# Hard-max attention on one core: key differences made by one VectorE subtraction and one store, in place of a negated first key, three stores and an accumulating DMA

## The chip, the cores and the metric

One core of a Trainium2 chip runs the program. The metric is the device time in microseconds, the median of several executions. Engines are named as in the profile: PE (TensorE, matmuls), PEld (its weight loads), DVE (VectorE), ACT (ScalarE), POOL (GpSimd) and SP (SyncE). DMAs that POOL issues go through the queue q0 (software_dynamic), those that SP issues through q1 (hardware_dynamic).

## The reference

```python
B, Sq, Sk, D = 4, 4096, 4096, 128          # q, k, v: randn, float32

def reference(q, k, v):
    logits = np.matmul(q, k.transpose(0, 2, 1))
    best = np.argmax(logits, axis=-1)
    b_idx = np.arange(q.shape[0])[:, None]
    return v[b_idx, best, :].astype(np.float32)
```

For each query the output is the row of `v` whose key has the largest dot product with it.

## The kernel before

**Screening.** The 4 x 4096 queries are worked as 128 tiles of 128 queries, `NQT` = 32 tiles to a batch `b`. Keys are taken in groups of four. For each tile `t`, PE multiplies the queries with sums and differences of the keys of a group (`kT`, fp16), ACT takes absolute values (`A`, L222) and one rectified half (`E`, L235), PE adds `A` back in, and DVE folds the two halves into one word per group (`fold`, L248, tile `W`). A word holds the score in its upper half and the group's number in its lower half. `top` (L252) takes the eight largest words of each query. The score is a measure that the largest dot product in the group can't exceed by much, so the best word names the group in which the winner lies.

**Dots.** `gather` (L264 and L270) decodes the best word into `cand` on DVE and lets POOL issue one indirect DMA for each tile. It fetches for each of 128 queries three rows from a scratch array in DRAM, `k16[b]`: the differences of keys 1, 2 and 3 of the group to key 0, in fp16, 384 values in all. They land in a tile `kg`, of which there are `NKG` = 6. `dots` (L288 to L298) multiplies them with the queries and sums, and `pick` (L308 to L321) chooses the key by the largest of 0 and the three. POOL then fetches the row of `v` (`vr`, L328), and SP stores it (L333). Groups of tiles whose result is too near to call are flagged and worked exactly, once for the first half of the tiles, beside the loop, and once at the end (L468 on).

**The loop and its order.** The order on every engine is written out by hand: a loop over `it` from 0 to 127 issues loads, one unit of transposed keys for the next batch (`unit_k`), the matmuls of tile `it` and the end of tile `it - 1` (`screen`), the fold of tile `it - 1`, one step of each piece of work in progress (`step`), the maximum of tile `it - 2` (`top`), another step, and last the gathers (`gathers`, `issue`). Each engine works its list in order, and each DMA queue is issued in order. POOL's list has the loads of the keys and queries of later batches (`load_part`, L66 and L69), the gathers of `kg` and `vr`, and L94. SP's list has the stores of `k16`, `rec` (L341, the eight words of each query) and the output, and the transposing DMAs of the queries (`turn_q`, L196).

**How `k16` is made.** The keys of a batch lie in `natk[b % 2]` as fp16, 16 consecutive keys to a partition, in two halves `h`. For batch 0, `put_k` (L71 to L78) subtracts key 0 from keys 1 to 3 of each group on DVE, into `kd`, and SP stores the half in one DMA. For batches 1 to 3 the work is split in the loop:

- at tiles 9 and 13 of the batch before (`it % NQT in (9, 13)`, L787), between `fold` and `step`, `put_first` writes minus key 0 to `kd[:, h, :, 0, :]` on DVE (L84), and SP stores this into all three places of each group in `k16` (L87, three DMAs)
- at tiles 12 and 16 (L789), `add_rest` lets POOL issue one DMA from `natk` to `k16` with `accum_op=OP.add` (L94), which adds keys 1 to 3 to what lies there.

In both ways `k16` holds the same three differences. `kd` has two halves, so a store of one half has to be done before the next batch writes that half again. The first reader of `k16[b]` is the gather for the first tiles of batch `b`.

Of the kernel before, what the change touches and what calls it, by code (L numbers as in the profile page):

```python
# [15 lines left out]
OP = mybir.AluOpType  # L16
# [13 lines left out]
def kernel(ctx, tc, q, k, v, out):  # L30
    nc = tc.nc
    B, Sq, D = q.shape
    Sk = k.shape[1]
    P = 128
    NQT = Sq // P
# [21 lines left out]
    k16 = [dr.tile([Sk, 96], FP16, name=f"k16_{b}") for b in range(B)]  # L57
    kT = [bp.tile([P, Sk], FP16, name=f"kT{i}", tag=f"kT{i}") for i in range(2)]
    qT = [bp.tile([P, Sq], FP16, name=f"qT{i}", tag=f"qT{i}") for i in range(2)]
    natk = [bp.tile([P, 2, 16, P], FP16, name=f"natk{i}", tag=f"natk{i}") for i in range(2)]  # L60
    kd = bp.tile([P, 2, 4, 3, P], FP16, name="kd", tag="kd")
# [9 lines left out]
    def put_k(b, h):  # L71
        if b >= B:
            return
        src = natk[b % 2][:, h].rearrange("p (g f) d -> p g f d", f=4)
        nc.vector.tensor_tensor(out=kd[:, h], in0=src[:, :, 1:4, :], in1=src[:, :, 0:1, :].to_broadcast([P, 4, 3, P]),
                                op=OP.subtract)
        kb16 = k16[b].rearrange("(h p n) d -> p h (n d)", p=P, n=16)
        nc.sync.dma_start(out=kb16[:, h], in_=kd[:, h].rearrange("p g f d -> p (g f d)"))  # L78

    def put_first(b, h):  # L80
        if b >= B:
            return
        src = natk[b % 2][:, h].rearrange("p (g f) d -> p g f d", f=4)
        nc.vector.tensor_scalar(out=kd[:, h, :, 0, :], in0=src[:, :, 0, :], scalar1=-1.0, scalar2=None, op0=OP.mult)  # L84
        kb16 = k16[b].rearrange("(r x) d -> r (x d)", x=4).rearrange("(h p g) (f d) -> p h g f d", h=2, p=P, f=3)
        for f in range(3):
            nc.sync.dma_start(out=kb16[:, h, :, f, :], in_=kd[:, h, :, 0, :])  # L87

    def add_rest(b, h):
        if b >= B:  # L90
            return
        src = natk[b % 2][:, h].rearrange("p (g f) d -> p g f d", f=4)
        kb16 = k16[b].rearrange("(r x) d -> r (x d)", x=4).rearrange("(h p g) (f d) -> p h g f d", h=2, p=P, f=3)
        nc.gpsimd.dma_start(out=kb16[:, h].rearrange("p g f d -> p g (f d)"), in_=src[:, :, 1:4, :].rearrange("p g f d -> p g (f d)"),  # L94
                            accum_op=OP.add)

    def load_part(b, i):
        if b >= B:
            return
        if i < 8:  # L100
            load_k(b, i // 4, i % 4 * 4, i % 4 * 4 + 4)
        else:
            load_q(b, (i - 8) * NQT // 8, (i - 7) * NQT // 8)
# [91 lines left out]
    def turn_q(b, x, y):  # L195
        nc.sync.dma_start_transpose(out=qT[b % 2][:, x * P:y * P].rearrange("p (t r) -> p t r", r=P),  # L196
                                    in_=natq[b % 2][:, x:y, :].rearrange("p t d -> p (t d)"))
# [42 lines left out]
    def screen(t):  # L240
        dpart(t, 0)
        spart(t - 1, 0)
        dpart(t, 1)
        spart(t - 1, 1)

    def fold(t):
        E, ps = E_t.pop(t)
        nc.vector.scalar_tensor_tensor(out=W_t[t % NW].bitcast(I16)[:, 1::2], in0=ps, scalar=QSCALE, in1=E,  # L248
                                       op0=OP.mult, op1=OP.max)

    def top(t):
        nc.vector.max(out=TOP[:, t, :], in_=W_t[t % NW].bitcast(FP32))  # L252
# [433 lines left out]
    def step(it):  # L686
        quick = it >= TAIL
        waiting = [s for s in live if s["kind"] == "dots" and ready(s, it)]
        quota = 2 if len(waiting) > 1 else 1
        again = []  # L690
        for s in list(live):
            if s["kind"] == "dots":
                if quota and advance(s, it, False):
                    quota -= 1
            elif advance(s, it, False) and (quick or s["kind"] == "flags"):
                again.append(s)
        for s in again:
            if s in live:
                advance(s, it, False)
# [17 lines left out]
    def issue(it):  # L717
        n = 0
        clock[0] = it
        put_out(it)  # L720
        behind = len([g for g in near_q if g not in marks]) > (2 if it >= TAIL else 4)
        while near_q and (n < 1 + behind or near_q[0] in marks):
            g = near_q.pop(0)
            n += g not in marks
            g()
        if fast and it >= rest[0]:
            fast.pop(0)()
            rest[0] = it + 2
            n += 1
        if it < 16:  # L730
            take_late(2 if n == 0 and len(late_q) > 4 else 1)
            return
        b, qt = it // NQT, it % NQT
        busy = 0.4 if 10 <= qt < 18 and b + 1 < B or 18 <= qt < 26 and b + 2 < B else 0.0
        room[0] = min(room[0] + 2.42 - busy, 3.0) - n
        for i in range(2):
            if room[0] >= 1 and late_q:
                take_late(1)
                room[0] -= 1
# [3 lines left out]
    def gathers(t):  # L743
        for c, (t0, t1) in enumerate(chunks):
            m = 4 if t1 <= T - 56 else 2 if t < T - 2 else 1
            if t0 <= t < t1 and (t - t0) % m == m - 1:
                gather(c, t - m + 1, m)
            if t == t0:
                start(pick(c, t0, t1), "pick", c)
        if t % 8 == 7:  # L750
            put_rec(t - 7, t + 1)
        if t == SEGS[1] - 1:
            last = [c for c, x in enumerate(chunks) if x[1] == t + 1][0]
            start(flag_segment(0, t + 1, lambda: ("cnt", last) in done, lambda: ("out", last) in done), "flags")
# [3 lines left out]
    for b in range(1, B):  # L758
        x = b * NQT
        units += [(x - 1, x - NQT + (6 + 3 * i // 2 if b == 1 else 1 + 2 * i), unit_k, b, i) for i in range(16)]  # L760
    for it in range(T):
        b, qt = it // NQT, it % NQT
        if it < 8:
            load_part(1, it)
        elif 10 <= qt < 18:
            load_part(b + 1, qt - 2)
        elif 18 <= qt < 26:
            load_part(b + 2, qt - 18)
        open_units = [u for u in units if u[1] <= it]
        if open_units:  # L770
            u = min(open_units)
            units.remove(u)
            assert it <= u[0]
            u[2](*u[3:])
        if it == 1:
            turn_q(0, 4, 8)
        if it in (1, 2, 3):
            turn_q(0, it * 8, it * 8 + 8)
        elif qt >= 16 and qt % 2 == 0 and b + 1 < B:
            turn_q(b + 1, (qt - 16) * 2, (qt - 14) * 2)  # L780
        if it > 0:
            screen(it)
        if it >= 1:
            fold(it - 1)
        if it == 1:
            put_k(0, 1)
        if it % NQT in (9, 13):  # L787
            put_first(it // NQT + 1, it % NQT // 13)
        if it % NQT in (12, 16):  # L789
            add_rest(it // NQT + 1, it % NQT // 16)  # L790
        step(it)
        if it >= 2:
            top(it - 2)
        step(it)
        if it >= 2:
            gathers(it - 2)
        issue(it)
# [75 lines left out]
```

## Time and profile before

| what | value |
|---|---|
| median of 3 runs | 452.23 us (452.08 to 452.82) |
| the profiled execution | 452.23 us, of which 450.3 us are the span from first to last instruction |
| folds (L248), maxima (L252) on DVE | 128 x 1301 ns, 128 x 1222 ns |
| A (L222), E (L235) on ACT | 256 x 1041 ns, 128 x 1033 ns |
| matmuls of 512 columns on PE | 1536 x 379 to 380 ns, pipelined |
| gathers of `kg` on POOL (L270) | 128 x 1009 ns to issue, median 2.7 us to landing |
| `k16` stores L87 (SP) and accumulates L94 (POOL) | 18 of 128 KB, median 3.4 us to landing; 6 of 384 KB, 5.8 us |

The profile is of one execution. "Busy" counts what the engine works on; POOL shows 0.30 us between two DMA issues even where nothing holds it. Instructions on an engine overlap a little, so the spacing of their starts is less than their durations. The 40 slices of the span show how the engines fill:

```profile
PE   7999999999999997999998888889889999991100
PEld 4444444444444443444443333433333333330100
DVE  2688999999999969999999999999999999999840
ACT  2999999999999996999999788899988999991000
POOL 8323667887768888877678787777677777777772
```

One digit is a tenth of full in 11.3 us. The last three slices are the end of the program: the dots of the last tiles, the flagged rows and the last stores.

### The profile page before, as it was taken

The numbers are of one execution on the slowest core, as the hardware profiler recorded it, in microseconds if no ns is written. First come the engines' busy times: TensorE is split into PE (matmuls) and PEld (weight loads), VectorE is DVE, ScalarE is ACT, GpSimd is POOL, SyncE is SP. The second block draws the span as 40 slices with busy tenths as digits, with TensorE's granted clock in tenths as the row PEclk, the third lists the DMA queues.
The fourth block names the chain that finished last, engine by engine and source line by source line (L and its number), as shares of the span: only waits on it lengthen the run. The fifth ranks groups of instructions, "written<-read, shape, count | busy, mean of one in ns | idle before, by whom it ended". The sixth has DMA issues, their size and how long they took to land.

```text
span 450.3 us, 6327 instructions
## 1 busy us (share of the span) xinstructions
PE 381.8 (85%) x1830; PEld 168.8 (37%) x1830; DVE 408.8 (91%) x767; ACT 377.9 (84%) x437; POOL 322.6 (72%) x351
## 2 busy tenths in 40 slices
PE   7999999999999997999998888889889999991100
PEld 4444444444444443444443333433333333330100
DVE  2688999999999969999999999999999999999840
ACT  2999999999999996999999788899988999991000
POOL 8323667887768888877678787777677777777772
PEclk9999999999999998999999999999999999998555
DMA  7943989473326999663236985273232332323331
GB/s 124 197 102 75 158 137 135 104 124 94 95 73 138 168 141 154 130 125 86 82 86 143 157 142 117 62 156 89 83 100 64 102 95 79 92 87 87 103 100 44
DMA packets 55429, 49.88 MB, mean 111 GB/s; under 512 B 34504, under 2 KB 46027, under 8 KB 55392
## 3 DMA queue, kind: packets, MB, share of 16 engines
q0 software_dynamic: 21920, 33.33, 38.0%
q1 hardware_dynamic: 33472, 16.13, 15.0%
q8 instruction: 14, 0.23, 0.2%
q14 instruction: 23, 0.19, 0.1%
HBM read 39.59 MB, written 14.55 MB: 120 GB/s over the span
## 4 chain that ended last, share of the span: by engine, by line
ACT 30%; DVE 19%; issue 18%; PE 17%; DMA 8%; POOL 7%; POOLq 0%; ACTq 0%; DVEq 0%; SPq 0%
ACT A L222 24%; DVE TOP L252 7%; PE psn L213 6%; ACT E L235 6%; PE psn L232 5%; DVE W L248 5%; PE pd L213 4%; DMA kg<-k,cand 3%; POOL vr L328 3%; POOL kg L270 2%; DVE prod L288 2%; DMA natk<-in_k_dram 2%; POOL natq L69 1%; DMA FK<-in_k_dram,gb_e 1%; POOL k L94 1%
## 5 line engine op out<-in xcount | busy, mean ns | idle before, releaser
L222 ACT ACTIVATE A<-pd 128x1024 f16<-128x1024 f32 x256 | 259.6, 1041 | 10.4 <-PE pd L213 8.9
L270 POOL DMA_INDIRECT kg<-k,cand x128 | 129.1, 1009 | 74.1 <-DVE cand L264 40.1
L248 DVE SCALAR_TENSOR_TENSOR W<-psn,E 128x1024 int16<-128x1024 f32 x128 | 166.5, 1301 | 7.3 <-ACT E L235 5.3
L213 PE MATMUL psn<-kT,qT 128*128 128x512 f16 x512 | 152.3, 379 | 15.1 <-ACT A L222 6.2
L328 POOL DMA_INDIRECT vr<-in_v_dram,win x128 | 131.9, 1030 | 39.7 <-issue 35.3
L213 PE MATMUL pd<-kT,qT 128*128 128x512 f16 x512 | 152.5, 380 | 8.1 <-ACT A L222 6.5
L213 PEld LDWEIGHTS <-qT 128*128 128x128 f16 x1024 | 98.2, 97 | 156.4 <-issue 67.1
L252 DVE MAX8 TOP<-W 128x8 f32<-128x1024 f32 x128 | 156.4, 1222 | 0.0
L232 PE MATMUL psn<-A,identh 128*128 128x512 f16 x512 | 152.6, 379 | 0.0
L235 ACT ACTIVATE E<-psn 128x1024 int16<-128x1024 f32 x128 | 132.3, 1033 | 6.7 <-PE psn L232 6.1
L232 PEld LDWEIGHTS <-identh 128*128 128x128 f16 x512 | 49.7, 97 | 61.1 <-issue 0.6
L288 DVE TENSOR_TENSOR prod<-kg,natq 128x768 f16<-128x768 f16 (+1 forms) x65 | 35.4, 544 | 6.4 <-DMA kg<-k,cand 6.3
L193 ACT ACTIVATE kT<-uk 128x256 f16<-128x256 f32 x48 | 20.1, 419 | 3.7 <-PE uk L190 3.7
L293 DVE TENSOR_TENSOR p<-prod 128x384 f16<-128x384 f16 (+2 forms) x47 | 19.9, 423 | 0.1
L298 DVE TENSOR_REDUCE D<-p 128x6 f32<-128x192 f16 (+2 forms) x47 | 19.2, 410 | 0.1
L66 POOL DMA_DIRECT2D natk<-in_k_dram x27 | 15.9, 594 | 0.9 <-POOLq L857 0.8
L69 POOL DMA_DIRECT2D natq<-in_q_dram x27 | 16.4, 608 | 0.0
L189 PE MATMUL uk<-identh,natk 128*128 128x128 f16 x96 | 16.0, 220 | 0.0
L486 PE MATMUL fp_e<-n_e,tri 128*128 128x1 f32 x2 | 0.6, 363 | 16.8 <-DVE n_e L484 16.8
L296 DVE TENSOR_TENSOR p<-p 128x192 f16<-128x192 f16 (+2 forms) x47 | 13.3, 285 | 0.1
L190 PEld LDWEIGHTS <-natk 128*128 128x128 f16 x96 | 9.4, 98 | 7.1 <-issue 4.5
L189 PEld LDWEIGHTS <-natk 128*128 128x128 f16 x96 | 9.5, 99 | 5.7 <-issue 0.3
(149 smaller groups left out, 136.3 us busy)
## 6 DMA issues: line engine op xcount, KB each, us to landing
out_dram<-vr SPq DMA_DIRECT2D x32, 256.0 KB, 2.4
natq<-in_q_dram POOLq DMA_DIRECT2D x26, 128.0 KB, 4.4
natk<-in_k_dram POOLq DMA_DIRECT2D x24, 128.0 KB, 4.6
k<-kd SPq DMA_DIRECT2D x18, 128.0 KB, 3.4
k<-natk POOLq DMA_DIRECT2D x6, 384.0 KB, 5.8
kg<-k,cand POOLq DMA_INDIRECT x128, 2.7
vr<-in_v_dram,win POOLq DMA_INDIRECT x128, 2.6
natq<-in_q_dram POOLq DMA_DIRECT2D x1, 768.0 KB
```

Of the source, the lines that this page charges most:

```text
L69: nc.gpsimd.dma_start(out=natq[b % 2][:, x:y], in_=q[b].rearrange("(p t) d -> p t d", p=P)[:, x:y])
L189: nc.tensor.matmul(out=o, lhsT=natk[b % 2][:, h, 4 * m + x, :], rhs=identh, start=True, stop=False)
L193: nc.scalar.activation(out=kT[b % 2][:, c:c + 256], in_=ps, func=AF.Copy)
L213: nc.tensor.matmul(out=ps[:, n * 512:(n + 1) * 512], lhsT=qT[b % 2][:, qt * P:(qt + 1) * P], rhs=kT[b % 2][:, u * 1024 + n * 512:u * 1024 ...
L222: nc.scalar.activation(out=A, in_=ps, func=AF.Abs)
L232: nc.tensor.matmul(out=ps[:, n * 512:(n + 1) * 512], lhsT=identh, rhs=A[:, n * 512:(n + 1) * 512], start=False, stop=True)
L235: nc.scalar.activation(out=E, in_=ps, func=AF.Relu, scale=QSCALE)
L248: nc.vector.scalar_tensor_tensor(out=W_t[t % NW].bitcast(I16)[:, 1::2], in0=ps, scalar=QSCALE, in1=E, op0=OP.mult, op1=OP.max)
L252: nc.vector.max(out=TOP[:, t, :], in_=W_t[t % NW].bitcast(FP32))
L270: near_q.append(lambda j=j: nc.gpsimd.indirect_dma_start(out=kg[:, j].rearrange("p f d -> p (f d)"), out_offset=None, in_=k16[t0 // NQT], ...
L288: nc.vector.tensor_tensor(out=prod[:, i:i + h], in0=kg[:, i:i + h], in1=natq[b % 2][:, x + i - b * NQT:x + i + h - b * NQT, :].unsqueeze(2 ...
L328: late_q.append(lambda j=j: nc.gpsimd.indirect_dma_start(out=vr[:, j, :], out_offset=None, in_=v_flat, in_offset=IOA(ap=win[:, i + j:i + j ...
```

## The change

`put_first` and `add_rest` are taken out. At the tiles at which `put_first` was called, `put_k` is called, as for batch 0; the calls at tiles 12 and 16 go.

```diff
-    def put_first(b, h):
-        if b >= B:
-            return
-        src = natk[b % 2][:, h].rearrange("p (g f) d -> p g f d", f=4)
-        nc.vector.tensor_scalar(out=kd[:, h, :, 0, :], in0=src[:, :, 0, :], scalar1=-1.0, scalar2=None, op0=OP.mult)
-        kb16 = k16[b].rearrange("(r x) d -> r (x d)", x=4).rearrange("(h p g) (f d) -> p h g f d", h=2, p=P, f=3)
-        for f in range(3):
-            nc.sync.dma_start(out=kb16[:, h, :, f, :], in_=kd[:, h, :, 0, :])
-
-    def add_rest(b, h):
...
-        nc.gpsimd.dma_start(out=kb16[:, h].rearrange("p g f d -> p g (f d)"), in_=src[:, :, 1:4, :].rearrange("p g f d -> p g (f d)"),
-                            accum_op=OP.add)
...
         if it % NQT in (9, 13):
-            put_first(it // NQT + 1, it % NQT // 13)
-        if it % NQT in (12, 16):
-            add_rest(it // NQT + 1, it % NQT // 16)
+            put_k(it // NQT + 1, it % NQT // 13)
```

The function that is now called for all batches:

```python
    def put_k(b, h):
        if b >= B:
            return
        src = natk[b % 2][:, h].rearrange("p (g f) d -> p g f d", f=4)
        nc.vector.tensor_tensor(out=kd[:, h], in0=src[:, :, 1:4, :], in1=src[:, :, 0:1, :].to_broadcast([P, 4, 3, P]),
                                op=OP.subtract)
        kb16 = k16[b].rearrange("(h p n) d -> p h (n d)", p=P, n=16)
        nc.sync.dma_start(out=kb16[:, h], in_=kd[:, h].rearrange("p g f d -> p (g f d)"))
```

For each of batches 1 to 3 and each half, one DVE operation of 128 x 512 values becomes one of 128 x 1536, three DMAs of SP become one, and one DMA of POOL goes.

## The prediction, made before the changed kernel ran

> **What bounds the kernel now.** I read the whole page first, then the idle time of each engine, then the timelines of VectorE and GpSimd around the lines that change, then the DMA queues in the same stretch.
>
> The page, span and engines:
>
> ```profile
> span 450.3 us, 6327 instructions
> ...
> PE 381.8 (85%) x1830; PEld 168.8 (37%) x1830; DVE 408.8 (91%) x767; ACT 377.9 (84%) x437; POOL 322.6 (72%) x351
> ```
>
> DVE is the busiest. Whether it is the bound is told by its waits. Here are all of them between 43 and 413 us (columns: who waited for what, us in total, times, longest):
>
> ```profile
> DVE prod L288 <- DMA kg<-k,cand: 6.3, 5, 3.9
> DVE W L248 <- PE psn L232: 0.2, 1, 0.2
> DVE W L248 <- issue: 0.2, 1, 0.2
> ```
>
> So in 370 us DVE waits for PE and ACT for 0.4 us, and for gathered keys (`kg`) for 6.3 us. It never idles otherwise. PE and ACT are nearly full in the first half (ACT 46.00 of 46.00 us from 41 to 87 us), but a fold on DVE starts later and later after its inputs are ready: about 0.2 to 0.6 us up to tile 27, 1.3 us at tile 50, 2.1 us at tile 73. Once that lag is there, the end of the tile loop is the sum of DVE's work and DVE's waits, and the 37 us tail after 413 us starts from it. Every number below is therefore DVE time after 43 us.
>
> The five waits are at 169.20 (3.90 us), 193.44 (0.78), 267.68 (0.59), 280.79 (0.27) and 293.82 (0.78). The largest, on the DVE timeline (start, duration):
>
> ```profile
> 163.92 1.31 DVE L248 SCALAR_TENSOR_TENSOR W<-psn,E 128x1024 int16<-128x1024 f32 x1
> 165.11 0.19 DVE L315 TENSOR_TENSOR sel<-near,iota 128x32 f32<-128x32 f32 x1
> 169.20 0.56 DVE L288 TENSOR_TENSOR prod<-kg,natq 128x768 f16<-128x768 f16 x1 [3.90 <-DMA kg<-k,cand]
> 169.67 1.22 DVE L252 MAX8 TOP<-W 128x8 f32<-128x1024 f32 x1
> ```
>
> and POOL's timeline just before it:
>
> ```profile
> 160.44 1.35 POOL L94 DMA_DIRECT2D k<-natk  x1
> 162.09 1.07 POOL L270 DMA_INDIRECT kg<-k,cand  x1 [0.30 <-issue]
> ```
>
> L94 is the accumulating DMA that the change removes. The last gather of the group is issued directly behind it in the same queue; the chain of waits gives that gather 7.08 us (162.09 to 169.17), where the page's median is 2.7. The DMA view of 163 to 167 us shows what it stands behind:
>
> ```profile
> q0 software_dynamic: 508, 0.43, 110.2%
> q1 hardware_dynamic: 430, 0.10, 41.9%
> ```
>
> GpSimd's queue q0 keeps all 16 DMA engines full: the 512 pieces of the accumulate, 768 B each, at 84 to 260 ns a piece, then the gather.
>
> **What the change costs.** Six times (tiles 9, 13, 41, 45, 73, 77) `put_first` becomes `put_k`. The rows for `kd`:
>
> ```profile
> L84 DVE TENSOR_SCALAR kd<-natk x6: 270/277/369, 41.1 to 247.7; 128x512 f16<-128x512 f16 x6
> L75 DVE TENSOR_TENSOR kd<-natk x2: 946/948/950, 9.0 to 17.9; 128x1536 f16<-128x1536 f16 x2
> ```
>
> L75 is the very operation that is added, in this kernel's prologue. Operations overlap, so occupancy is start to start: L84 starts at 41.13 and the next one at 41.32, 0.19 us (0.29 once, at 147.28). L288 lasts 0.55 and occupies 0.46 to 0.47, so 0.08 to 0.09 overlaps; 0.95 less 0.08 is 0.87 us. Each replacement costs 0.87 - 0.19 = 0.68 us, six cost 4.0 us.
>
> Not all is paid. The pair at tiles 9 and 13 falls where DVE still has idle time: 0.25 us at 43.00, 0.12 at 51.83, 0.17 at 87.23, some 0.55 in all with the gaps of 0.05. That cover takes 0.55 of 1.36 and leaves 0.8; the cost is 1.36 if the cover is gone, 0 if tiles 14 to 28 have more slack than the gaps show. The pairs at tiles 41, 45 and 73, 77 have no cover: 2.7 us. Sum: 0.8 + 2.7 = **+3.5 us**, bounds 2.7 and 4.1.
>
> **What it removes.** On POOL six L94 at 1.36 us with a 0.30 gap each, 10 us. POOL does not set the end, but between 126 and 220 us it runs without a gap over 0.6 us, so everything behind the L94 at 144.78 moves 1.7 us forward, and behind the one at 160.44 3.3 us. On SP, 18 stores L87 (128 KB, pieces of 256 B, 0.5 to 1.4 us of issuing each) become six of 384 KB in 3 KB pieces; L78, the same store in the prologue, takes 0.34 us of SP and lands in 5.7 us. `rec` stores and transposes queued behind on SP are issued some 1.5 us earlier. On q0, six accumulates of 3 to 4 us of all engines' time vanish. The built program has the same order otherwise on all five engines: no gather or product moves to another tile. L75 waits for the same loads as L84 and for the store before it from the same half of `kd`, 32 tiles back; L84's longest wait entry in DVE's queue is 0.05 us, and behind it stand only a maximum and a piece of the dots. The first gather from the next batch's `k16` now waits for those stores instead of the accumulate, some 20 tiles after them: nothing.
>
> Wait by wait. At 169.20: the gather moves from 162.09 to about 158.8. Even if it stood in the queue behind a natq load as others do and took 5.4 us (the longest in the view of `kg`, of the gathers for which it gives a landing), it lands at 164.2; DVE, later by 0.8 + 1.36, wants it at 167.4. Gone: -3.90. At 267.68: the L94 at 261.58 stood before the gather at 263.24, which took 4.34 us; 1.7 us sooner is enough for a wait of 0.59. Gone: -0.59. At 193.44 and 280.79 no accumulate is near: there it is POOL's lead that counts. At 188.06 POOL is still in its gapless stretch and gains 3.3 us where DVE gains 1.8, so 1.5 against a wait of 0.78; at 276 it gains 1.7 relative to DVE (it last waited for DVE at 258.70) against 0.27. I take both as gone, -1.05; bounds 0 and -1.05. At 293.82 POOL waited for DVE at 286.21, after all L94, so nothing changes: 0, bounds 0 and -0.78. Sum: **-5.5 us**, bounds -4.5 and -6.3.
>
> New DVE waits elsewhere: the same gathers come earlier and DVE later, so margins grow up to 160 us. Where DVE gains, after 169, PE and ACT must stay ahead of it: in the profile the lag of the folds falls to 0.37 us at tile 56 after the stall and DVE still does not wait; without the stall it would be 3.4 us at tile 50. Zero.
>
> A rule that speaks against the change is in the Trainium skill, "SBUF — State Buffer", section "SBUF: two separate sides": VectorE operations with two SBUF inputs and GpSimd operations that read SBUF exclude each other for the whole instruction, and the loser waits. This trace has a mild form: the gather at 255.83 that meets products of two SBUF inputs takes 1.60 us, against a median of 0.96. By the rule each subtraction could hold POOL up to 0.95 us, 5.7 in six, against 10 us removed there; on DVE, which would have to lose the lock to matter, no product row exceeds 0.58, so by the row it is zero.
>
> **Sum.** 3.5 - 5.5 = -2.0 us. The profiled execution took 452.23 us (450.3 of span, 1.9 around it) and the median of the runs shown is the same 452.23, so: **450.2 us**. Own range: from 452.23 + 2.7 - 6.3 = 448.6 to 452.23 + 4.1 - 4.5 = 451.8.
>
> **Rivals.**
> *Only the two waits behind an accumulate go.* For it: at 188 to 194 us the queue q1 (transposes) holds 47% of the engines, so POOL's lead may not help. Against: that lead is twice the wait. Price: 3.5 - 4.5 = -1.0, 451.2 us.
>
> *The transposes hold the gathers, not the accumulate* (slower). Place: 162 to 169 us. The transposes issued at 160.99 on SP stand behind a `rec` store that waits for DVE's `cand`, so they move with DVE, and q1 has 42% in the window above; their landing is 7.4 us there against 5.3. If they keep the last gather in flight until DVE wants it, no wait shrinks and the subtraction is paid in full: 452.23 + 3.5 = 455.7 us. It begins once that gather, issued near 158.8, takes over 8.6 us (to 167.4), and has its full price at 12.5. Against: at 267 us the same pattern has a wait only because of 1.7 us of queue, and after 61.08 an accumulate with little q1 traffic fills q0 the same way (108.8% from 62 to 66 us).
>
> *DVE is later only in part.* If the first pair is hidden wholly and the wait at 293.82 goes as well: 448.6 us; for it, ACT is full up to 87 us. Against: DVE's gaps there sum to 0.55 only.
>
> *Nothing comes of it.* The subtraction, beside busier queues than in the prologue, takes 1.15 rather than 0.95 us (+1.2 in six) and the small waits stay: 452.4 us. Against: 61 products of the same kind in the loop average 0.55 us.
>
> **How the numbers follow.** Main forecast 0.58, two waits only 0.16, hidden pair 0.08, nothing 0.08, slower 0.10. About 0.2%, 0.9 us, is what a measurement of this kernel can tell from no change, so the edges are 451.3 and 453.1. Faster: main but for its upper end (0.54), half of the second case, which lies on the edge (0.08), and the hidden pair (0.08): 0.70. Same: the two remainders (0.04 and 0.08) and most of the fourth case (0.06): 0.18. Slower: its rival and the rest of the fourth, 0.12. The range leaves out the slower rival alone: 448.6 to 452.6, the upper end a little over the fourth case.
>
> **What would show it.** L75 six more times at 0.95 us and 0.87 start to start; no DVE wait near 166 us over 0.5; DVE waits after 43 us in sum about 0.8; the last gather before the product near 165 us issued near 159 and landed in under 5 us; POOL's busy time down 8 us; folds' lag at tile 50 near 3.4 us. I am wrong if DVE waits for PE or ACT after 169 us, if L75 takes over 1.1 us in the loop, or if a gather still lands late with no accumulate before it.

## The result, and the profile after

| | median | span of the profiled execution |
|---|---|---|
| before | 452.15 us (451.40 to 452.82, 4 runs) | 450.3 us |
| changed | 458.83 us (457.69 to 460.42, 4 runs) | 455.6 us |

The ratio is 1.0151, 95% interval 1.0111 to 1.019: the changed kernel is slower by 6.7 us in the medians, and by 5.3 us of span between the two profiled executions. Medians and ratios, here and below, are taken over the runs within 1.5% of the fastest of their kernel on the same chip. The page of the changed kernel, its span and engines:

```profile
span 455.6 us, 6311 instructions
...
PE 381.9 (84%) x1830; PEld 168.5 (37%) x1830; DVE 412.5 (91%) x767; ACT 378.5 (83%) x437; POOL 316.2 (69%) x345
```

DVE works 3.7 us more, POOL 6.4 us less. The waits of DVE from 43 to 413 us (who waited for what, us in total, times, longest):

```profile
DVE prod L271 <- DMA kg<-k,cand: 2.3, 1, 2.3
DVE W L231 <- PE psn L215: 0.5, 2, 0.3
```

The waits for gathered keys fell from 6.3 us to 2.3. So more work and fewer waits about cancel, and the 5.3 us are elsewhere. To see where, take the copy `bs_e` on DVE, the first step of the closing part for the flagged rows, on DVE's timeline (start, duration). Before:

```profile
424.49 0.16 DVE L489 COPY bs_e<-fp_e 128x1 f32<-128x1 f32 x1 [0.61 <-PE fp_e L486]
```

and after:

```profile
424.27 0.16 DVE L472 COPY bs_e<-fp_e 128x1 f32<-128x1 f32 x1 [0.61 <-PE fp_e L469]
```

Up to there the changed kernel is 0.2 us *ahead*. The last DMA that POOL issues, a scatter of corrected rows to the output, is also 0.2 us ahead. POOL's timeline, before:

```profile
444.75 1.03 POOL L556 DMA_INDIRECT out_dram<-FV,rowk_e  x1 [3.31 <-DMA out_dram<-vr]
```

and after:

```profile
444.54 1.03 POOL L539 DMA_INDIRECT out_dram<-FV,rowk_e  x1 [3.31 <-issue]
```

What is left is the program's last line, which has only queue instructions that no "busy" counts. One of them is DRAIN, with which an engine closes its list. Its rows (duration in ns, least, median, most; first and last start in us), POOL's before:

```profile
L868 POOLq DRAIN  x3: 46/109/4977, 444.5 to 450.1; - x3
```

and after:

```profile
L849 POOLq DRAIN  x3: 46/109/10489, 444.3 to 455.4; - x3
...
L849 DVEq DRAIN  x2: 10/14/17, 440.8 to 455.1; - x2
```

POOL's closing DRAIN takes 10.49 us (from 444.31) where it took 4.98 (from 444.52). After it the program ends within 0.85 us in both. It is longer by 5.5 us, what comes before it is shorter by 0.2: together the 5.3 us of the span.

It doesn't just wait for the last DMA. That scatter is issued while the DRAIN runs, and in the trace the last packet of POOL's queue ends 2.10 us after the DRAIN's start in both kernels; the DRAIN goes on for 2.87 us after that before, and for 8.39 us in the changed kernel.

The Trainium skill, "VectorE: DVE Perf Modes", section "The DRAIN you can't avoid", speaks of DRAINs from the opening and closing parts that the runtime puts around a program: about 12 ns, constant, on all five engines. DVE's row above (10 to 17 ns) agrees; POOL's longest is nearly nine hundred times that, and not constant. Here the measurement decides.

One thing the two profiles don't explain: the four times of the changed kernel are spread over 2.7 us, those before over 1.4, and the profiled execution is the shortest of its four. Some 1.4 us of the 6.7 stay unplaced.

### The profile page after: what moved, and what is told of

It reads as the page before. It is cut to its first block, busy times and chain, and to the rows that moved or that the text cites. A ratio compares the mean times of both kernels' runs of the same rounds, so it can differ in the third digit from the quotient of the medians.

```text
span 455.6 us, 6311 instructions
## 1 busy us (share of the span) xinstructions
PE 381.9 (84%) x1830; PEld 168.5 (37%) x1830; DVE 412.5 (91%) x767; ACT 378.5 (83%) x437; POOL 316.2 (69%) x345
## 4 chain that ended last, share of the span: by engine, by line
DVE 22%; ACT 16%; PE 15%; issue 11%; DMA 3%; POOL 1%; POOLq 0%; ACTq 0%; DVEq 0%; SPq 0%
ACT A L205 11%; DVE TOP L235 8%; DVE W L231 6%; PE psn L196 6%; PE psn L215 5%; ACT E L218 4%; PE pd L196 4%; DMA vr<-in_v_dram,win 2%; DVE prod L271 2%; DVE p L276 1%; DMA kg<-k,cand 1%; DVE p L279 1%; DVE D L281 1%; DVE kd L75 1%; POOL vr L311 1%
```

## The experiments

The theory after reading the two traces was that the closing DRAIN's length depends on what POOL has sent through its own DMA queue, which the change altered, and not on what the last DMAs do. The rivals were that the accumulating DMA itself has to be there, that the length follows the time of the end, and that VectorE's dearer operation is the loss after all.

On the chips of the experiments the tile loop of every kernel, the one before too (512 to 533 us there), was stretched by waits of the folds for PE and ACT, with a granted clock of 0.88 to 0.93 against 0.94 to 0.95; so times are compared only between kernels that ran beside each other on one chip, while the DRAIN, which repeats to 0.02 us, is read from each trace.

To compare kernels, "entries" means the pieces of a POOL DMA that one of the 16 DMA engines moves, and one more for its completion. That is an estimate from the queue's row: six accumulates of 512 pieces add 3168 packets, 528 each, so 33 for each of 16 engines. For other DMAs the row has fewer packets, since one record joins several pieces (those of a copy of 512 pieces are of 4608 and 1536 B, six and two pieces); their entries are counted from the pieces all the same, which no row shows to be right.

### The accumulate, a plain copy, or a tiny DMA

Three kernels are the changed one with six extra POOL DMAs into an unused scratch array, at the places where `add_rest` was called (tiles 12 and 16 of a batch).

```diff
+        if it % NQT in (12, 16):
+            extra(it // NQT + 1, it % NQT // 16)
# e1: accumulate, 384 KB
+        nc.gpsimd.dma_start(out=j16[:, h]..., in_=src[:, :, 1:4, :]..., accum_op=OP.add)
# e2: the same without accum_op
# e3: 128 pieces of 4 bytes
+        nc.gpsimd.dma_start(out=junk[:, 2 * b + h:2 * b + h + 1], in_=HARD)
```

Expected of the accumulate aside:

> The changed kernel (subtraction and one store) plus the six accumulating DMAs of the kernel before at their old places on POOL, but into a scratch array that nobody reads; GpSimd issues the same DMAs as before. The changed kernel's loop ended 0.2 us earlier than before's (bs_e at 424.27 against 424.49) and its last GpSimd drain took 10.5 us against 5.0. Theory 1 (the closing drain depends on how much GpSimd has put through its own DMA queue): drain back at about 5 us. Theory 2 (it depends on accumulating DMAs having run): also about 5 us. Theory 3 (it depends on where the program ends in time, or on chance): 10 us or more. For the loop: if the accumulate is what held the gather at tile 48, a DVE wait of 2 us or more near 165 us comes back although the subtraction is there, and the loop ends 2 to 4 us later than in the changed kernel; if the transposes held it, no such wait.

Of the copy aside:

> The same with plain copies instead of accumulates, same shape (512 pieces of 768 B), six times, into scratch. Theory 1: drain about 5 us, as in the run with accumulates. Theory 2: drain 10 us. Loop: a plain copy does not read its destination, so its pieces should take less than the 84 ns seen; the wait near 165 us should be smaller than with the accumulate, 0 to 2 us.

Of the six tiny DMAs:

> The changed kernel plus six tiny GpSimd DMAs (128 x 4 B to scratch) at the places of the accumulates: same number of GpSimd DMAs as before, a quarter of the pieces, no data. Theory 1 as a matter of the number of DMAs: drain 5 us. Theory 1 as a matter of pieces: something between or other than 5 and 10.5. Theory 2 and 3: 10 us or more. Loop as in the changed kernel within 1 us.

The closing line, with the accumulates aside:

```profile
L860 POOLq DRAIN  x3: 46/109/4980, 499.1 to 504.9; - x3
```

With the plain copies:

```profile
L859 POOLq DRAIN  x3: 46/109/3959, 506.7 to 511.5; - x3
```

With the tiny DMAs:

```profile
L857 POOLq DRAIN  x3: 46/257/2988, 498.3 to 502.5; - x3
```

All three cut it, and the tiny ones most. So neither an accumulation nor a large transfer is needed. Nor is it the number of POOL's DMAs alone, which is six more in all three: the 5 us expected of the copies too came only with the accumulates. With these it is the figure of the kernel before to 3 ns, though everything else is the changed kernel: the DRAIN follows POOL's DMAs and nothing else in the diff. The times, side by side, were 507.43 (accumulates), 513.96 (copies), 504.85 (tiny) and 531.74 (before), single runs that can't rank them.

Beside them ran a kernel with VectorE's price doubled, the subtraction run twice in the loop:

```diff
-        nc.vector.tensor_tensor(out=kd[:, h], ...
+        for _ in range(2 if b else 1):
+            nc.vector.tensor_tensor(out=kd[:, h], ...
```

> The changed kernel with the subtraction of batches 1 to 3 done twice (the second overwrites the same values): 6 x 0.87 = 5.2 us of DVE more, nothing else moved. If DVE's time after 43 us is what sets the loop's end, the first instruction after the loop (bs_e) comes 4 to 5 us later than 424.3; if DVE has slack, less than 2. Theory 1 and 2: the drain stays at 10 us or more; theory 3 (time at which the program ends): it may change.

It took 529.84 us, 2 us under the kernel before beside it, with the DRAIN at 10.49 us. One run says nothing on 5 us here; the DRAIN says that a VectorE operation doesn't move it.

### Timed again

The tiny DMAs, the accumulates and the double subtraction were run again, the tiny DMAs several times.

> The changed kernel plus six tiny GpSimd DMAs, as in the run before that gave a closing drain of 2.99 us against 10.49 in the changed kernel, now timed against the kernel before. If the drain alone made the changed kernel slow (10.49 - 4.98 = 5.5 us and more in its slower runs), this one must be no slower than the kernel before: 457.7 - 7.5 = 450.2 us, ratio 0.994 to 1.000. If something else made it slow (store, transposes, the later subtraction), ratio 1.005 or more.

> Accumulates into scratch beside the changed kernel once more, for the loop, which in the first run was stretched everywhere (PE waits, clock 0.92). Drain 4.98 us. If the accumulate held the gather, a DVE wait of 2 to 4 us near 165 us and the loop's end (bs_e) near 426 to 428; if not, no such wait and 424.3.

> Subtraction twice, once more for the loop. Drain 10.49 us, as in the changed kernel and in the first such run, since GpSimd's DMAs are the same. If DVE's time sets the loop's end: bs_e 4 to 5 us later than 424.3, total near 462; if DVE has slack, bs_e under 426.

> The changed kernel plus six tiny GpSimd DMAs, timed once more, in the hope of engines that run as in the kernel before's own profile (the earlier timing ran with all loops stretched to 510 us and gave a ratio of 0.989). Theory (the closing drain is what made the change slow): drain 2.99 us, total 457.7 - 7.5 = 450.2 us, ratio to before 0.994 to 1.000. Rival (the loop pays for the subtraction): ratio 1.005 or more.

> Changed kernel plus the six accumulates into scratch. Drain 4.98 us. Loop: the wait of the second product of tiles 40 to 43 (near 167 us) comes back with 1.5 to 4 us if the accumulate in front of the gather made it; 0 if the transposes did. Total then 452 to 456 us.

With the tiny DMAs the kernel took 0.9893 (0.983 to 0.9957) of the kernel before, and on another chip 0.9856 (0.9727 to 0.9986), a little less than the 0.994 to 1.000 expected, into which both intervals reach; the DRAIN was 2.98 us in both. The other three gave one time each: accumulates 516.16 and 508.13 us (DRAIN 4.98 in both), double subtraction 531.97 (DRAIN 10.49). Beside them the kernel before took 514.13 to 530.60 and 512.33 to 533.08 us on the two chips, so these three times rank nothing.

The accumulates aside also answer the old question of the wait of 3.90 us. They write to an array that nobody reads, so the product doesn't need them. In the first such run, POOL's timeline has the same order as before the change:

```profile
174.80 1.35 POOL L86 DMA_DIRECT2D junk<-natk  x1
176.45 1.07 POOL L262 DMA_INDIRECT kg<-k,cand  x1 [0.30 <-issue]
```

and DVE's:

```profile
182.11 0.56 DVE L280 TENSOR_TENSOR prod<-kg,natq 128x768 f16<-128x768 f16 x1 [1.47 <-DMA kg<-k,cand]
```

The wait is back, with 1.47 us; 1.05 in the second repeat, none in the first. In every kernel without an accumulate this product doesn't wait, though the transposes are all there, and six plain copies of the same bytes leave no wait there either. The accumulate ahead of the gather in the queue makes that wait, as far as DVE is early enough to notice; on these chips it is later.

### What is counted

The theory at this point: the DRAIN grows with the entries that have piled up, and at some count, called the wrap here, the pile starts anew. Then entries added anywhere in the program should move it up, and past the wrap down. So the next kernels added a number of them: two or seven copies of 2048 pieces at the start of the loop (258 and 903 entries), the six tiny DMAs in the kernel *before*, and one, three and 36 tiny DMAs.

```diff
# f4 (it <= 2), g3 (it <= 7)
+            if 1 <= it <= 2:
+                nc.gpsimd.dma_start(out=junk[it][:, :, 0:32], in_=natk[0][:, 0, :, 0:32])
# g4: extra() as in e3, in the kernel before
# h1
+        if it == 44:
+            extra(2, 0)
# h2
+        if it in (44, 48, 76):
+            extra(it // NQT + 1, it % NQT // 16)
# h3
+        if 1 <= it <= 9:
+            for i in range(4):
+                extra(i // 2, i % 2)
```

> The changed kernel plus two GpSimd DMAs early on (tiles 1 and 2, where GpSimd idles), each of 2048 pieces of 64 B, that is 128 pieces and one semaphore write for each of 16 engines: 258 more entries in each engine's queue, in 2 DMAs. Theory: GpSimd keeps the entries it has written until a wrap, and the closing drain walks what has piled up since the last wrap; the changed kernel ends just before a wrap, six tiny DMAs (54 entries) put it just past. From the runs: 144 entries more cost 0.97 us (six DMAs of 8 pieces against 32 an engine), so 204 entries past the six tiny ones gives 2.99 + 1.4 = 4.4 us. Rival: the drain depends on the number of DMAs or on the length of GpSimd's program: then two DMAs leave it at 10.5 us or give some value not tied to 4.4.

> Seven of the early DMAs of 2048 pieces of 64 B instead of two: 903 entries more for each engine than in the changed kernel, 849 more than with the six tiny DMAs. The two gave a drain of 4.13 us for 204 entries past the tiny ones, the semaphore instruction in the tail 0.845 us against 0.383, 2.3 ns an entry. Theory (entries pile up to a wrap): that instruction 0.38 + 849 x 2.3 ns = 2.3 us and the drain near 10 us again, or, if the wrap comes earlier than that, both small again (under 1 us, under 4 us). Rival (each DMA beside the first few makes it shorter, or program length decides): drain near 3 to 4 us with the semaphore instruction unlike both.

> The kernel before plus the same six tiny DMAs (54 entries more). Theory of entries: the drain grows a little, from 4.98 to 5.2 to 5.6 us, the semaphore instruction from 1.05 to 1.15 to 1.2. Rival (six more DMAs simply help): drain near 3 us as in the changed kernel with them.

> The changed kernel plus one tiny GpSimd DMA (9 entries in each engine's queue, the semaphore write included). Theory (entries pile up until a wrap that lies between 0 and 54 entries further): either the drain is still at 10.5 to 10.6 us and the semaphore instruction at 2.40 to 2.42, or both have fallen to their floor, 2.98 and under 0.4; nothing between. Rival (each further DMA shortens the drain, six by 7.5 us): 9.2 us.

> Three tiny ones (27 entries). Theory: again either about 10.6 us or the floor, and not higher than with one only if it has fallen. Rival: half way, 6.7 us.

> 36 tiny ones, early in the loop (324 entries): 270 entries past the six tiny ones. From 2 ns an entry in the semaphore instruction and 4 ns in the drain for each of its: semaphore instruction 0.38 + 0.54 = 0.9 to 1.0 us, drain 4.3 to 5.0 us. Rival (more DMAs never hurt): drain at its floor, 2.98 us. If 36 tiny ones and seven of 129 entries follow one line, the count that matters is not the number of entries alone.

The closing line of three tiny DMAs:

```profile
L857 POOLq DRAIN  x3: 46/109/2900, 505.8 to 509.5; - x3
```

of one tiny DMA:

```profile
L857 POOLq DRAIN  x3: 46/109/10574, 525.1 to 536.2; - x3
```

of the kernel before with six:

```profile
L875 POOLq DRAIN  x3: 46/109/5388, 514.7 to 520.9; - x3
```

and of seven large copies:

```profile
L852 POOLq DRAIN  x3: 46/257/4446, 521.9 to 527.4; - x3
```

All in one table. INC is a second instruction of POOL's queue in the closing part (INC_SWDGE_SEM, 8 to 11 us earlier), which has a length of its own in every trace:

| kernel | entries added | INC, us | DRAIN, us |
|---|---|---|---|
| changed | 0 | 2.40 | 10.49 |
| + one tiny (h1) | 9 | 2.42 | 10.57 |
| + three tiny (h2) | 27 | 2.45 | 2.90 |
| + six tiny (e3) | 54 | 0.38 | 2.99 |
| + six copies (e2) | 198 | 0.78 | 3.96 |
| + two large copies (f4) | 258 | 0.85 | 4.13 |
| + 36 tiny (h3) | 324 | 1.01 | 4.77 |
| + seven large copies (g3) | 903 | 0.92 | 4.45 |
| + six accumulates (e1) | see text | 1.03 | 4.98 |
| before | | 1.05 | 4.98 |
| before + six tiny (g4) | 54 more | 1.16 | 5.39 |

Nine entries raise the DRAIN by 0.08 us, 18 more drop it by 7.7 us, and from there it climbs again: 0.81 us for the 126 entries from 198 to 324, or 6.4 ns each, and 0.41 us for 54 in the kernel before, 7.6 ns each. Between neighbouring rows the rise is uneven, 2.9 ns an entry from 198 to 258 and 9.7 from 258 to 324, so the count of pieces isn't exactly what matters. INC rises about 2 ns an entry in the same rows, and falls by 2.07 us between 27 and 54 added. With three tiny DMAs INC still stands before its fall and the DRAIN already behind it. On the theory, the wrap lies between the two instructions, among the last DMAs of the program, and the changed kernel ends 9 to 27 entries short of it, by the accident of its count. The fall is shown; that something piles up and starts anew is argued from it.

From the fall of 7.7 us and 6.4 to 9 ns an entry, the pile that is cleared at a wrap would be some 850 to 1200 entries, an estimate. The Trainium skill has two statements near this: "DMA: Bandwidth & Descriptors", section "Terms", says that GpSimd writes descriptors of 16 bytes to rings in SBUF, and "SBUF — State Buffer", section "SBUF size: 192, 224, or 256?", that 16 KiB of each partition are kept for them. That would make 1024 entries a partition, an estimate from these pages, and lies within that estimate; no run here shows that the DRAIN clears such a ring.

Two rows don't fit a plain count. Seven large copies should have come near 10 us or, past the wrap, under 4, and gave 4.45. And six accumulates give 1.02 us more than six copies of as many pieces, so an accumulate counts for more. A count of packets fits no better: three tiny DMAs and two large copies each add 96 to the queue's row, and gave 2.90 and 4.13 us. What exactly is counted, and how long the full period is, stays open.

### The result of it, timed

Last, three kernels ran on one chip beside the kernel before, several times each: the changed kernel itself, with three tiny DMAs, and with the subtraction twice.

> The changed kernel itself, beside the next one on the same chip, for a timed difference of the two. Drain 10.49 us. Its time less that of the version with three tiny DMAs: 7.6 us (10.49 - 2.90), if the drain is all that parts them.

> The changed kernel plus three tiny GpSimd DMAs (tiles 44, 48, 76), which put the wrap just ahead of the end. Drain 2.90 us. On a chip whose loop runs as in the first profiles 450 us against 452.2 before and 457.7 to 460.4 of the changed kernel; on a stretched one the same differences within the spread, ratio to before 0.98 to 1.00. Rival (the drain is hidden by something else that ends the program): no difference to the changed kernel.

> The changed kernel with the subtraction twice, timed on the same chip. If DVE's time sets the loop's end, 4 to 5 us over the changed kernel; if the loop waits for other things there, less than 2.

| kernel | median, us | of all runs | ratio to before (95%) | DRAIN, us |
|---|---|---|---|---|
| before | 518.56 (10 runs) | 521.52 (17) | 1 | |
| changed | 524.61 (6 runs) | 524.61 (6) | 1.0159 (1.0093 to 1.0224) | 10.49 |
| + three tiny DMAs | 516.17 (9 runs) | 517.51 (12) | 0.9945 (0.9893 to 0.9997) | 2.90 |
| + second subtraction | 528.22 (4 runs) | 528.22 (4) | 1.0205 (1.0138 to 1.0272) | 10.50 |

The closing line of the changed kernel:

```profile
L849 POOLq DRAIN  x3: 46/109/10492, 508.6 to 519.7; - x3
```

and with three tiny DMAs:

```profile
L857 POOLq DRAIN  x3: 46/109/2903, 509.0 to 512.7; - x3
```

Three DMAs of 512 bytes, which nobody reads, take 8.4 us off the median (7.1 with all runs counted), and 7.6 us off the DRAIN. From the DRAIN's start to the end of the program the traces have 11.34 and 4.24 us, so 7.1 us of the 7.6 can show. The short DRAIN ends at 511.95, before SP gets to its own closing DRAINs; in the changed kernel SP is there at 511.9 and POOL's DRAIN ends at 519.12. SP's row with the three tiny DMAs:

```profile
L857 SPq DRAIN  x3: 7/7/13, 512.1 to 512.4; - x3
```

The interval of the kernel with three tiny DMAs doesn't overlap that of the changed kernel, and it is the fastest of the four; over the one before it gains 0.55%, with an interval that just keeps clear of 1. On the first chip its span would be 455.6 - 7.1 = 448.5 us, an estimate, since it ran only where loops were stretched. A second subtraction adds 3.6 us in the medians (six times 0.87 would be 5.2), but the intervals overlap, so its price in time isn't settled. Nor is what the changed loop is worth there: the changed kernel is 6.1 us slower than the one before with a DRAIN that should be 5.5 us longer, and the 0.6 us left over are well within the interval.

## Why the prediction was wrong, by its own steps

**The step that failed: "the 37 us tail after 413 us starts from it".** The tail was taken as a fixed length behind the loop, so that the whole forecast was a sum of DVE time. It holds an instruction whose length depends on what POOL has sent through its DMA queue, and the change removes six of them, each with 512 pieces. The removal was priced on POOL's busy time and on the queue's engines, where it is a gain, and not at the end, where it cost 5.5 us. With 5.5 us for the DRAIN, and the 1.8 us by which the loop missed its forecast (below), 450.2 would have been 457.5; the profiled execution took 457.69. It could have been found: 4.98 us of POOL's DRAIN was in the last line of the program before, outside all busy time, and asking what a tail's last 5 us consist of would have put a term of unknown size on the sum. Its sign could not be read from that one trace.

**VectorE's price: right.** L75 in the changed kernel:

```profile
L75 DVE TENSOR_TENSOR kd<-natk x8: 934/948/975, 8.9 to 247.4; 128x1536 f16<-128x1536 f16 x8
```

Start to start, the six replacements occupy 5.16 us where the negations took 1.26: +3.90, forecast 4.0. The rival in which it takes 1.15 us in the loop is out. The cover of 0.55 us for the first pair didn't show: of the 3.90 us, 3.80 are left in DVE's time, without its idle time, from the fold of tile 2 to `bs_e`.

**The waits behind an accumulate: right.** -3.90 and -0.59 were forecast. The product that waited 3.90 us runs without any:

```profile
165.18 1.35 DVE L231 SCALAR_TENSOR_TENSOR W<-psn,E 128x1024 int16<-128x1024 f32 x1
166.37 0.23 DVE L298 TENSOR_TENSOR sel<-near,iota 128x32 f32<-128x32 f32 x1
166.47 0.61 DVE L271 TENSOR_TENSOR prod<-kg,natq 128x768 f16<-128x768 f16 x1
```

Those at 267.68, 280.79 and 293.82 are gone too, the last against the forecast of no change. The rival that the transposes hold these gathers is out: it needed this wait to stay. (The pieces of the accumulate took 82 to 1291 ns in the trace, half of them at most 84, not the 84 to 260 that the prediction reads; its full queue doesn't depend on that.) DVE's waits for PE are 0.5 us, where no new ones were forecast; one of 0.33 us, at 254.86, is the sign of being wrong that the prediction named for the time after 169. The lag of the folds at tile 50, named as a sign at 3.4 us, is about 1.0 us by the end of `E` (1.4 before).

**POOL's lead: mis-sized, and with it the wait at 193.44.** The step was that "everything behind the L94 at 144.78 moves 1.7 us forward, and behind the one at 160.44 3.3 us". The gather behind the second moved from 162.09 to 161.18, 0.9 us. The sum was too large, and the price of the subtraction on POOL was left out of it.

The sum: the L94 at 144.78 starts while the load at 144.22 ends, without the gap of 0.30 us. From that load to the gather behind L94 are 2.25 us before, and 0.91 us without it (144.90 to 145.81), so one L94 frees 1.34 us, not 1.7.

The price: the prediction said that each subtraction could hold POOL up to 0.95 us, and took nothing off POOL's lead for it. Before, the gather issued beside the first negation of this pair:

```profile
135.44 1.14 POOL L270 DMA_INDIRECT kg<-k,cand  x1 [0.30 <-issue]
```

and after, the subtractions of this pair on DVE and the issues of POOL beside them:

```profile
135.18 0.97 DVE L75 TENSOR_TENSOR kd<-natk 128x1536 f16<-128x1536 f16 x1
135.44 1.80 POOL L253 DMA_INDIRECT kg<-k,cand  x1 [0.30 <-issue]
147.97 0.97 DVE L75 TENSOR_TENSOR kd<-natk 128x1536 f16<-128x1536 f16 x1
148.40 1.68 POOL L311 DMA_INDIRECT vr<-in_v_dram,win  x1 [0.30 <-issue]
```

The first is 0.66 us longer than before, the second 0.68 longer than the same issue before (149.21, 1.00 us). Together they take the whole 1.34 us: the next group's first gather stands at 151.15 in *both* traces. The pair at tiles 73 and 77 does the same (1.81 and 1.54 us); beside the first pair POOL issues nothing. It isn't chance: over the traces of all kernels with a single subtraction, 30 of the 31 such issues that start with 0.6 us or more of a subtraction still to go took 1.52 to 1.82 us, against medians of 0.96 (`kg`) and 1.00 (`vr`), and those that start with under 0.25 us to go 1.00 to 1.33. The one exception (1.00) started 0.02 us after its subtraction, which then took 1.01 us. The added time is about what is left of the subtraction, so the rule that the prediction quoted does show here, at 0.5 to 0.85 us a time; the case it took for a mild form, at 255.83, is a `vr` issue, to be held against 1.00 us. POOL's busy time fell by 6.4 us and not by 8. The L94 at 160.44 frees 1.3 us, of which a gather at 157.56 that took 1.39 us against 0.99 takes 0.4.

Then the gather for the wait at 193.44:

```profile
187.39 1.18 POOL L253 DMA_INDIRECT kg<-k,cand  x1 [0.30 <-issue]
```

It was issued at 188.06 before, so POOL gained 0.67 us here, where 3.3 were forecast. DVE gained more, since its 3.90 us wait is gone: the fold ahead of the product starts at 188.86 instead of 191.28.

```profile
188.86 1.30 DVE L231 SCALAR_TENSOR_TENSOR W<-psn,E 128x1024 int16<-128x1024 f32 x1
190.06 0.17 DVE L298 TENSOR_TENSOR sel<-near,iota 128x32 f32<-128x32 f32 x1
192.53 0.56 DVE L271 TENSOR_TENSOR prod<-kg,natq 128x768 f16<-128x768 f16 x1 [2.30 <-DMA kg<-k,cand]
```

From issue to product the gather takes 5.14 us, 5.38 before: it isn't slower, DVE only comes 2.4 us earlier and gives most of that back. 0.78 + 2.42 - 0.67 = 2.53 would be the wait, 2.30 was measured. The forecast was 0, so the waits for gathered keys fell by 4.0 us instead of 5.5, and DVE's idle time as a whole, from the fold of tile 2 to `bs_e`, by 3.7.

**The sum.** +3.80 and -3.71 instead of +3.5 and -5.5: from the fold of tile 2 to `bs_e` the loop loses 0.1 us where it was forecast to gain 2.0. The changed kernel was 0.3 us ahead at that fold already, which leaves the 0.2 at `bs_e`. This falls short even of the rival in which only the two waits behind an accumulate go, since the wait near 193 us grew. With the old DRAIN that would have been about 452.0 us, no change that a measurement can tell. The range reached 452.6 and so left out the result because the tail had no term in it.

## What to carry to other kernels

Take the end of a program apart like any other stage: ask for its closing line, and compare the tails of two kernels separately from their loops. Where GpSimd issues DMAs, a change in their count or shape can move the end, here by up to 7.7 us and either way, so read the closing DRAIN before a loop is blamed, and, where the end sits just short of the fall, add or drop a few small DMAs. Before everything on an engine is moved forward by what is removed, work out from start to start what the removal frees, and look at what will run beside that engine's instructions: here two issues of POOL beside the new subtractions lost all that a removed DMA had freed.

## What the runs showed that was not expected

- GpSimd's closing DRAIN took 2.90 to 10.57 us in programs that differ in a few of its DMAs, falling by 7.7 us between 9 and 27 entries added and rising by 6 to 8 ns an entry over longer stretches.
- It is the same to 0.02 us in five executions with the same POOL DMAs (10.49 to 10.50 us), behind loops of very different length (spans of 455.6 to 529.9 us): it doesn't follow the time at which it starts.
- An accumulating DMA of 512 pieces counts more in it than a copy of 512 pieces (4.98 against 3.96 us for six).
- A DMA that GpSimd issues early in a VectorE subtraction of 128 x 1536 values (0.95 us) took 1.52 to 1.82 us to issue, against 0.96 to 1.00.
